# A streaming SiLU-gate kernel: first load cut in four, implied waits dropped, another closing wait

## The chip, the cores and the metric

The kernel runs on one core of a Trainium2 chip. The metric is device time in microseconds. Three runs of the kernel before gave a median of 472.07 us (471.17 to 472.86). The profile is of one execution of 471.1 us, whose span (first to last instruction) is 469.2 us.

A core has compute engines with instruction queues of their own, of which this kernel uses ScalarE (ACT), VectorE (DVE) and, to issue transfers, SyncE (SP). Transfers between the main memory (HBM) and the on-chip memory (SBUF, 128 partitions) are carried by sixteen DMA engines. An instruction waits for others by semaphores; a transfer raises its semaphore when it has landed.

## The reference

The input x is 32 x 512 x 2048 in float32, 134.22 MB. Its last dimension is cut in halves; the first goes through SiLU and gates the second:

```
half_dim = x.shape[-1] // 2
x1, x2 = (x[..., :half_dim].copy(), x[..., half_dim:].copy())
silu_x1 = x1 * (1 / (1 + np.exp(-x1)))
return (silu_x1 * x2).astype(np.float32)
```

The output is 32 x 512 x 1024 in float32, 67.11 MB. Every element is read once and written once, with no reuse.

## The kernel before

The 16,384 rows are cut into 16 tiles of 128 x 8 rows: partition p of a tile holds eight consecutive rows, 64 KB of input and 32 KB of output, each contiguous in HBM. Two input tiles (xt0, xt1) and two output tiles (ot0, ot1) alternate. SiLU is done in place in the first half of each row of the input tile (line 61, ACT); the product goes to the output tile (line 65, DVE).

The order of the work on each engine is the order of the program text (a manual schedule); the framework adds the semaphore waits that follow from which instruction touches which tile.

- SP issues the loads (line 57), one transfer of 8.39 MB for each tile. Load 0 and load 1 go out at once; load i+2 waits until the multiplication of tile i has freed its input tile, and for load i on the same tile.
- ACT does the SiLU and issues the stores, after the multiplication of the same tile, so a store stands between two activations in its queue.
- DVE does the multiplications. Before one it waits for the SiLU of its tile, for the load of that tile, for the store that last read the output tile, and for an earlier multiplication.

Tile 0 is treated apart: SiLU and product run in four pieces of two rows (FIRST, line 11), and five stores take strided sets of partitions (OPENING, line 16): every fourth partition, those halfway between, and all odd ones, with their rows split. Tiles 1 to 14 are done in one piece each (lines 81 to 86), and the last tile in two halves (LAST, line 13), each with a store of its own.

At the end an empty instruction on SP (line 96) waits for the last transfers but one store and for the last product, so that the framework's closing drain has few waits left to make.

The lines that the change and the steps of the prediction touch are the helpers load, silu, mul and store (lines 56 to 70), the first loads (72 and 73) and the closing (96 to 98).

Of the kernel before, what the change touches and what calls it, by code (L numbers as in the profile page):

```python
# [1 line left out]

# [4 lines left out]


K = 8

FIRST = [(0, 2), (2, 4), (4, 6), (6, 8)]

LAST = [(0, 4), (4, 8)]


OPENING = [
    (slice(0, None, 4), slice(0, 2)),
    (slice(2, None, 4), slice(0, 4)),
    (slice(2, None, 4), slice(4, None)),
    (slice(0, None, 4), slice(2, None)),  # L20
    (slice(1, None, 2), slice(None)),
]
SYNC = mybir.DependencyInfo(mybir.DependencyClass.Sync, mybir.DependencyReason.DATA)


@with_exitstack
def kernel(
    ctx: ExitStack,
    tc: tile.TileContext,
    x: bass.AP,  # L30
    out: bass.AP,
):
    nc = tc.nc
    P = nc.NUM_PARTITIONS

    x_flat = x.flatten_outer_dims()
    out_flat = out.flatten_outer_dims()
    num_rows, in_cols = x_flat.shape
    half = in_cols // 2
    dt = x_flat.dtype  # L40
    n_tiles = num_rows // (P * K)
    assert n_tiles * P * K == num_rows

    x_view = x_flat.rearrange("(n p k) d -> n p k d", p=P, k=K)
    out_view = out_flat.rearrange("(n p k) d -> n p k d", p=P, k=K)

    in_pool = ctx.enter_context(tc.tile_pool(name="in_pool", bufs=1))
    out_pool = ctx.enter_context(tc.tile_pool(name="out_pool", bufs=1))
    xts = [in_pool.tile([P, K, in_cols], dt, name=f"xt{j}") for j in range(2)]
    ots = [out_pool.tile([P, K, half], dt, name=f"ot{j}") for j in range(2)]  # L50

    ctx.enter_context(tc.manual_schedule())

    dmas = []

    def load(i):
        dmas.append(nc.sync.dma_start(out=xts[i % 2], in_=x_view[i]))  # L57

    def silu(i, a, b):
        x1 = xts[i % 2][:, a:b, :half]  # L60
        nc.scalar.activation(out=x1, in_=x1, func=mybir.ActivationFunctionType.Silu)  # L61

    def mul(i, a, b):
        xt = xts[i % 2]
        return nc.vector.tensor_mul(  # L65
            out=ots[i % 2][:, a:b], in0=xt[:, a:b, :half], in1=xt[:, a:b, half:]
        )

    def store(i, a, b):
        dmas.append(nc.scalar.dma_start(out=out_view[i][:, a:b], in_=ots[i % 2][:, a:b]))  # L70

    load(0)
    load(1)
    for a, b in FIRST:
        silu(0, a, b)
        mul(0, a, b)
    for ps, ks in OPENING:
        dmas.append(nc.scalar.dma_start(out=out_view[0][ps, ks], in_=ots[0][ps, ks]))
    load(2)

    for i in range(1, n_tiles - 1):
        silu(i, 0, K)
        mul(i, 0, K)
        store(i, 0, K)
        if i + 2 < n_tiles:
            load(i + 2)

    i = n_tiles - 1
    for a, b in LAST:
        silu(i, a, b)  # L90
        last_mul = mul(i, a, b)
    for a, b in LAST:
        store(i, a, b)


    seen = nc.sync.nop()
    for ins in [*dmas[-12:-1], last_mul]:
        tc.add_manual_dep(seen.ins, ins.ins.name, SYNC, reason="the closing waits")


# [1 line left out]
_INS = ['x']  # L102
_OUTS = [((32, 512, 1024), 'float32')]


# [23 lines left out]
```

## Time and profile before

| what | value |
|---|---|
| median of three runs | 472.07 us |
| profiled execution, its time and span | 471.1 us, 469.2 us |
| DVE busy | 139.4 us (30%), 20 instructions |
| ACT busy | 114.1 us (24%), 21 instructions |
| SiLU of a whole tile, mean | 7.03 us |
| product of a whole tile, mean | 8.69 us |
| load, issue to landing, least and median | 21.7 us, 41.9 us |
| store of a whole tile, issue to landing, median | 49.1 us |

The load's least, 21.7 us, is load 0's, which has the DMA engines to itself. The others share them with stores, and a transfer that is issued while others are queued waits behind them, so these times are mostly queueing. The page gives for each engine the time in which it executes, for the DMA the share of sixteen engines' time that their packets took. The name SPq, ACTq or DVEq in a row means the engine's instruction queue: it waits, or issues a transfer, and the engine itself stays idle.

### The profile page before, as it was taken

Reading aid. Unit: us, or ns where it says so; the run is one execution under the profiler, and the core shown is the slowest. Engines: PE = TensorE matmul, PEld = TensorE weight load, DVE = VectorE, ACT = ScalarE, POOL = GpSimd, SP = SyncE. Lnnn points to the kernel's source line nnn. Section 1 sums busy time; section 2 is a strip of 40 time slices with the busy share of each in tenths; the row PEclk is TensorE's granted clock in tenths of the full one; section 3 lists DMA queues with packets and bytes.
Section 4 is the critical chain, followed back from the end, with each engine's and each line's share of the span. In section 5 each row is a group of like instructions: output and inputs, shape, how many; then the busy total and the mean of one; then the engine's idle time right before and its main releaser. Section 6 shows DMA issues by size and latency. Waiting matters only on the chain.

```text
span 469.2 us, 199 instructions
## 1 busy us (share of the span) xinstructions
DVE 139.4 (30%) x20; ACT 114.1 (24%) x21; POOL 0.2 (0%) x4
## 2 busy tenths in 40 slices
DVE  0070604207052060510606115060250702407061
ACT  1052305050140501405023050230503205032060
POOL 0000000000000000000000000000000000000000
DMA  8999999999999999999999999999999899999998
GB/s 358 447 469 425 397 453 399 405 492 402 447 402 492 402 402 447 486 408 402 447 425 469 402 444 405 447 447 413 436 492 436 369 447 486 408 448 399 422 430 358
DMA packets 4881, 201.34 MB, mean 429 GB/s; under 512 B 592, under 2 KB 592, under 8 KB 592
## 3 DMA queue, kind: packets, MB, share of 16 engines
q1 hardware_dynamic: 2304, 134.22, 66.3%
q10 hardware_dynamic: 2576, 67.11, 33.2%
q14 instruction: 1, 0.01, 0.0%
HBM read 134.22 MB, written 67.11 MB: 429 GB/s over the span
## 4 chain that ended last, share of the span: by engine, by line
DMA 80%; DVE 14%; ACT 2%; DVEq 1%; issue 0%; SPq 0%; ACTq 0%
DMA out_dram<-ot 62%; DMA xt<-in_x_dram 18%; DVE ot L65 14%; ACT xt L61 2%; DVEq L124 1%; DVEq L65 0%; SPq L57 0%; ACTq L61 0%
## 5 line engine op out<-in xcount | busy, mean ns | idle before, releaser
L65 DVE TENSOR_TENSOR ot<-xt 128x8192 f32<-128x8192 f32 (+2 forms) x20 | 139.4, 6984 | 319.8 <-DMA out_dram<-ot 200.2
L61 ACT ACTIVATE xt<-xt 128x8192 f32<-128x8192 f32 (+2 forms) x20 | 112.9, 5662 | 338.9 <-DMA xt<-in_x_dram 338.9
L61 ACT ACT_TABLE_LOAD x1 | 1.3, 1283 | 0.7 <-PEq L113 0.7
L113 POOL MEMSET const-bfloat16-1.0<- 128x1 bf16 x1 | 0.1, 102 | 0.0
L113 POOL MEMSET const-uint8-127<- 128x1 uint8 x1 | 0.1, 102 | 0.0
L113 POOL MEMSET const-float32-0.0<- 128x1 f32 x1 | 0.1, 99 | 0.2 <-issue 0.2
L113 POOL MEMSET const-float32-1.0<- 128x1 f32 x1 | 0.1, 99 | 0.0
## 6 DMA issues: line engine op xcount, KB each, us to landing
out_dram<-ot ACTq DMA_DIRECT2D x14, 4096.0 KB, 49.1
out_dram<-ot ACTq DMA_DIRECT2D x3, 2048.0 KB, 9.2
out_dram<-ot ACTq DMA_DIRECT2D x2, 512.0 KB, 17.1
out_dram<-ot ACTq DMA_DIRECT2D x1, 768.0 KB, 27.9
xt<-in_x_dram SPq DMA_DIRECT2D x16, 41.9
out_dram<-ot ACTq DMA_DIRECT2D x1, 256.0 KB, 10.8
```

What stands on the lines that cost most here:

```text
L61: nc.scalar.activation(out=x1, in_=x1, func=mybir.ActivationFunctionType.Silu)
L65: return nc.vector.tensor_mul(out=ots[i % 2][:, a:b], in0=xt[:, a:b, :half], in1=xt[:, a:b, half:])
L113: nc = _bacc.Bacc("TRN2", target_bir_lowering=False, num_devices=1)
L124: with _tile.TileContext(nc) as tc:
```

## The change

- Load 0 becomes four transfers (ARRIVING): every eighth partition from 0, every eighth from 4, every fourth from 2, and all odd ones, that is 16, 16, 32 and 64 partitions. Each has a semaphore of its own, and the first SiLU waits for all four. Load 1 is issued behind them on SP.
- Waits that another wait implies are declared unnecessary: a multiplication no longer waits for its load (its SiLU did), nor for older work on the same tiles; likewise loads and activations. Some waits on older transfers appear elsewhere, where the framework still asks for them.
- An activation on a tile of one column (warm) stands ahead of everything on ACT. That tile takes 4 bytes in each partition ahead of the output tiles, which come to lie 32 bytes further on.
- The closing has two empty instructions on SP instead of one: the first waits for the last SiLU, the second for what the old one waited for. The closing drain then has the last store itself to wait for.

```
+ARRIVING = [slice(0, None, 8), slice(4, None, 8), slice(2, None, 4), slice(1, None, 2)]
...
+    def implied(ins, others):
+        for other in others:
+            tc.declare_no_dep(ins.ins, other.ins, reason="another wait implies it")
     def load(i):
-        dmas.append(nc.sync.dma_start(out=xts[i % 2], in_=x_view[i]))
+        for ps in ARRIVING if i == 0 else [slice(None)]:
+            ins = nc.sync.dma_start(out=xts[i % 2][ps], in_=x_view[i][ps])
+            dmas.append(ins)
+            loads.setdefault(i, []).append(ins)
+            if i >= 2:
+                implied(ins, [*loads[i - 2], *silus[i - 2]])
     def silu(i, a, b):
...
+        if i >= 2:
+            implied(ins, [*silus[i - 2], *muls[i - 2]])
     def mul(i, a, b):
...
+        implied(ins, loads[i])
+        if i >= 2:
+            implied(ins, [*loads[i - 2], *silus[i - 2], *muls[i - 2]])
...
+    warm = in_pool.tile([P, 1], dt, name="warm")
+    nc.scalar.activation(
+        out=warm,
+        in_=nc.const_aps.tensor(0.0, (P, 1), dt),
+        func=mybir.ActivationFunctionType.Silu,
+    )
     load(0)
     load(1)
...
-    seen = nc.sync.nop()
-    for ins in [*dmas[-12:-1], last_mul]:
-        tc.add_manual_dep(seen.ins, ins.ins.name, SYNC, reason="the closing waits")
+    for group in ([last_silu], [*dmas[-12:-1], last_mul]):
+        seen = nc.sync.nop()
+        for ins in group:
+            tc.add_manual_dep(seen.ins, ins.ins.name, SYNC, reason="the closing waits")
```

More of the change, by code (lines that the diff above doesn't have):

```diff
@@ L54 @@
     dmas = []
+    loads, silus, muls = {}, {}, {}
+    def implied(ins, others):
+        for other in others:
+            tc.declare_no_dep(ins.ins, other.ins, reason="another wait implies it")
     def load(i):
-        dmas.append(nc.sync.dma_start(out=xts[i % 2], in_=x_view[i]))
+        for ps in ARRIVING if i == 0 else [slice(None)]:
[4 more added lines that the diff above has]
+                implied(ins, [*loads[i - 2], *silus[i - 2]])
     def silu(i, a, b):
         x1 = xts[i % 2][:, a:b, :half]
-        nc.scalar.activation(out=x1, in_=x1, func=mybir.ActivationFunctionType.Silu)
+        ins = nc.scalar.activation(out=x1, in_=x1, func=mybir.ActivationFunctionType.Silu)
+        silus.setdefault(i, []).append(ins)
+        if i >= 2:
+            implied(ins, [*silus[i - 2], *muls[i - 2]])
+        return ins
     def mul(i, a, b):
         xt = xts[i % 2]
-        return nc.vector.tensor_mul(
+        ins = nc.vector.tensor_mul(
             out=ots[i % 2][:, a:b], in0=xt[:, a:b, :half], in1=xt[:, a:b, half:]
         )
+        muls.setdefault(i, []).append(ins)
+        implied(ins, loads[i])
+        if i >= 2:
+            implied(ins, [*loads[i - 2], *silus[i - 2], *muls[i - 2]])
+        return ins
     def store(i, a, b):
         dmas.append(nc.scalar.dma_start(out=out_view[i][:, a:b], in_=ots[i % 2][:, a:b]))
+    warm = in_pool.tile([P, 1], dt, name="warm")
[4 more added lines that the diff above has]
+    )
     load(0)
@@ L89 @@
     for a, b in LAST:
-        silu(i, a, b)
+        last_silu = silu(i, a, b)
         last_mul = mul(i, a, b)
```

## The prediction

> **What bounds the kernel now.** I read the page's DMA rows first, because both compute engines are idle most of the time (DVE 30%, ACT 24% busy). The page, its slices and its DMA rows:
>
> ```profile
> DMA  8999999999999999999999999999999899999998
> ...
> q1 hardware_dynamic: 2304, 134.22, 66.3%
> q10 hardware_dynamic: 2576, 67.11, 33.2%
> ...
> HBM read 134.22 MB, written 67.11 MB: 429 GB/s over the span
> ```
>
> Loads (q1) take 66.3% and stores (q10) 33.2% of sixteen engines' time over the span: together 99.5%. Nothing in the middle can be won by compute; only the two ends of the span and the pace of the packets are left. So I read the pace by stretches next (the columns are length, busy time of DVE, ACT and POOL, clock, DMA share, GB/s):
>
> ```profile
> 1.15:22.50 21.35, 0.00 (x0) 0.87 (x2) 0.00 (x0) 1.00 1.05 442
> 22.50:76.60 54.10, 17.59 (x5) 21.37 (x6) 0.00 (x0) 1.00 1.00 426
> 76.60:192.60 116.00, 34.77 (x4) 28.12 (x4) 0.00 (x0) 1.00 1.00 434
> ...
> 424.90:469.20 44.30, 17.45 (x3) 7.12 (x2) 0.00 (x0) 1.00 0.93 402
> ```
>
> The steady pace is 434 GB/s. A transfer's bytes count where its packets start, so the first row reads high and the last low. The second row holds the five strided stores of tile 0, and at 426 GB/s it lost 54.10 x (1 - 426/434) = 1.0 us. Then the same view, cut finely at the start:
>
> ```profile
> 1.70:1.80 0.10, 0.00 (x0) 0.10 (x1) 0.00 (x0) 1.00 9.66 3277
> 1.80:1.95 0.15, 0.00 (x0) 0.15 (x1) 0.00 (x0) 1.00 8.03 2621
> 1.95:2.20 0.25, 0.00 (x0) 0.06 (x1) 0.00 (x0) 1.00 0.72 262
> 2.20:2.50 0.30, 0.00 (x0) 0.00 (x0) 0.00 (x0) 1.00 1.12 437
> 2.50:2.80 0.30, 0.00 (x0) 0.00 (x0) 0.00 (x0) 1.00 1.05 437
> ...
> 4.60:5.00 0.40, 0.00 (x0) 0.00 (x0) 0.00 (x0) 1.00 2.27 983
> 5.00:5.20 0.20, 0.00 (x0) 0.00 (x0) 0.00 (x0) 1.00 7.56 3277
> ```
>
> A load's packet is one partition's 65,536 bytes, so GB/s times length counts packets: 5, 6, 1, 2 and 2 start in the first five rows (sixteen engines, one each, spread over 1.1 us), and 6 and 10 second packets start at 4.60 to 5.20. At 434/16 = 27.1 GB/s an engine needs 2.42 us for a packet. Second packets start at about 5.05 in the mean, so the streams ran as if begun at 5.05 - 2.42 = 2.63, though the first packet started near 1.75: some 0.9 us of lag. Last, the chain of waits (start, us, what) and the timeline, for one round of the loop:
>
> ```profile
> 105.53 0.03 issue
> 105.56 0.02 DVEq L65
> ...
> 105.72 8.70 DVE ot L65
> 114.43 0.02 issue
> 114.45 49.09 DMA out_dram<-ot
> ```
>
> ```profile
> 114.44 0.33 SPq L57 DMA_DIRECT2D xt<-in_x_dram  x1
> 114.45 0.36 ACTq L70 DMA_DIRECT2D out_dram<-ot  x1
> 127.44 7.03 ACT L61 ACTIVATE xt<-xt 128x8192 f32<-128x8192 f32 x1 [22.01 <-DMA xt<-in_x_dram]
> ```
>
> The chain names the multiplication, but it is not the limit: when it ends and SP issues the next load at 114.44, the load before it has 13 us of packets left (its silu starts at 127.44). The queue never runs dry.
>
> **The change part by part.** The sum is against the profiled execution: span 469.2, time 471.1, that is 0.97 below the median of 472.07 and at the low end of its runs (471.17 to 472.86).
>
> *First load in four.* Transfers of 16, 16, 32 and 64 partitions replace one of 128; bytes and packets stay. The first carries one packet for each of sixteen engines instead of eight, so I expect the late starters (five after 1.95) to start with the early ones. The earliest second packets start between 4.60 and 5.00, say 4.7, and the mean was 5.05: if all engines follow the earliest, the streams gain 0.35 us. Ends: 0 (the spread is not due to the transfer's size) and 0.9 (the whole lag goes). I take 0.35, since it supposes only what the quickest engines already show. This gain would last: the engines have no idle time behind it to absorb it.
>
> The price of the strided pattern on a load is in no row, since every load now spans 128 partitions. The nearest row is the stretch of strided stores (every fourth partition, every second): 1.0 us for five of them, 0.2 each. Ends: 0, and by bytes 8.39/4.19 x 1.0 = 2.0 us. I take 0.2, one such loss: the first transfer begins inside the start-up lag, and the stores lost it between alternating reads and writes, which the first load is not.
>
> Three more SP issues at 0.33 to 0.42 us move load 1's issue from 1.15 to about 2.4. Its packets are needed when engines leave load 0's, near 21.6, so 19 us cover it; without cover it would be 1.2 us. The next SP wait, for load 2, ends on the fourth multiplication at 33.4 as now. The first silu waits for four semaphores instead of one, some 0.05 us for each wait by the DVEq gaps above; the 21 us of load 1 hide 0.15 us.
>
> *Waits dropped.* From the landed store at 105.53 to the multiplication at 105.72 are 0.19 us of semaphore waits; one of two waits goes, some 0.1 us a round, 14 rounds. Load packets cover it (13 us a round), so I count nothing; were the cover gone it would be 1.4 us. Who is late next is again the DMA engines.
>
> *Warm activation.* The table load stays at 0.73 to 2.01. By 7.03 us for 8192 elements and 1.90 for 2048, an activation has about 0.2 us of fixed cost; ACT is idle until 22.49. Nothing. The small tile shifts the output tiles by 32 bytes in each partition. No row has that shift; stores hold 33.2% of the engines' time, 156 us, so one part in a thousand of their pace would be 0.16 us either way. I take 0.
>
> *Closing.* The last store is issued at 459.13 and lands 9.2 us later, at 468.4; the tail after it is 0.8 us. One semaphore wait of 17 ns with its gap leaves that tail: 0.05 us (ends 0 and 0.1). The last silu's wait moves ahead, to an instruction that it reaches with the activations done since 453.8; it delays nothing.
>
> Sum: -0.35 + 0.2 - 0.05 = -0.2 us on 471.1, that is 470.9; on the median 471.9.
>
> **The rivals.** Within 0.3%, 1.4 us, a measurement of this kernel can hardly tell a change from none.
>
> *Engines meet in SBUF (slower).* Sixteen engines write sixteen partitions that lie eight apart. If two must share one way in, each packet takes twice 2.42 us, and in lockstep every engine meets the same in the second transfer. Price: two packets an engine, 4.84 us, so 476.7. If the third and fourth transfers meet too, eight packets: 19.3 us, 491.2. It decides once the sixteen-partition packets take a third longer (1.6 us over both, to outweigh the 0.2 gained). Against it: strided stores at half speed would have cost 4.19 MB / 217 GB/s - 4.19 / 434 = 9.7 us, and that stretch lost 1.0. For it: those stores are reads of SBUF, every fourth partition and not every eighth. I give 0.19 to two slow transfers, 0.08 to four.
>
> [...]
>
> *The strided price goes by bytes.* 2.0 us instead of 0.2: 473.7, just slower. For it: the stretch at 426. Against: its cost need not repeat when only loads run. 0.09.
>
> *The whole lag and the strided stores' loss go.* Starts at once (0.9), arrival in another order also frees the stretch of its 1.0, and the tail gives 0.1: 470.1, faster by 0.4%. For it: both losses are in the rows. Against: five stores are unchanged. Or the dropped waits count after all, 1.4 us: about 470.5. Together 0.21.
>
> **How the numbers follow.** My forecast of 471.9 has 0.43, its own range 471.0 to 473.0. Slower is 0.19 + 0.08 + 0.09 = 0.36, faster 0.21, within 0.3% 0.43. The range runs from 469.9 (the faster rival and a little) to 477.2 (two slow transfers with half the strided price); it leaves out the four slow transfers and the low tail, some 0.15.
>
> **What would show it.** Second packets starting together at 4.6 to 4.8 prove the gain at the start; a first silu near 22.2 proves that nothing was lost in load 0. A first silu near 27 shows two slow transfers, near 41 four, with 217 GB/s from 2 to 12 us. The loop's pace must stay at 434 and the wait before a multiplication shrink by 0.1 us with no change in the spacing of stores. I am wrong if load 0 lands late, or if the output tiles' shift changes the pace of the steady stretches.

## The result, and the profile after

The changed kernel takes 475.36 us in the median of six runs (475.25 to 475.51). The kernel before, in more runs than the prediction had, takes 471.12. The runs of the kernel before lie in two groups, most near 471.0 and the rest 0.6 to 2.1 us above, so its median moves by some tenths of a microsecond with the share of each. The ratio is 1.0085, with a 95% interval of 1.0075 to 1.0095: slower by 0.85%, about 4.2 us. The profiled execution took 475.34 us with a span of 473.6.

The slices of the page, first the rates of the kernel before, then the changed kernel's busy shares and rates. The DMA engines are as full as before and the bytes are the same, but the first slice moves 194 GB/s instead of 358. A share counts the time that packets take, so slow packets don't show in it.

```profile
GB/s 358 447 469 425 397 453 399 405 492 402 447 402 492 402 402 447 486 408 402 447 425 469 402 444 405 447 447 413 436 492 436 369 447 486 408 448 399 422 430 358
```

```profile
DMA  8999999999999999999998999999999999998998
GB/s 194 426 443 400 432 453 421 437 426 443 443 443 443 443 399 443 443 407 435 487 443 376 437 471 399 443 443 443 399 443 440 446 404 437 487 437 379 426 440 354
```

The start of the changed kernel, cut finely (length, busy DVE, ACT, POOL, clock, DMA share, GB/s counted where a packet starts; the rows left out between 3.30 and 14.60 are zero):

```profile
1.70:1.95 0.25, 0.00 (x0) 0.25 (x1) 0.00 (x0) 1.00 0.00 0
1.95:3.30 1.35, 0.00 (x0) 0.26 (x2) 0.00 (x0) 1.00 3.56 777
...
6.30:7.80 1.50, 0.00 (x0) 0.00 (x0) 0.00 (x0) 1.00 3.30 699
7.80:11.20 3.40, 0.00 (x0) 0.00 (x0) 0.00 (x0) 1.00 0.00 0
11.20:12.80 1.60, 0.00 (x0) 0.00 (x0) 0.00 (x0) 1.00 1.85 655
...
14.60:15.40 0.80, 0.00 (x0) 0.00 (x0) 0.00 (x0) 1.00 3.03 1311
```

GB/s times length, divided by 65,536 bytes, is 16 in each row that is not zero: the engines go in step. Their second packets start at 6.3 to 7.8 (before: 4.6 to 5.2), the third at 11.2 to 12.8, the fourth at 14.6 to 15.4. From the middle of one row to the middle of the next are 4.95 us for the second packet, which is the one of the second transfer, where 2.42 is the steady time (65,536 bytes at 434/16 GB/s); the third takes 3.0 and later ones 2.4. Sixteen packets of 65,536 bytes in 4.95 us are 212 GB/s, half of 434. The first transfer fares the same, from about 2.4 to 7.05 with the start-up lag in it. The other two run at full pace but for the mixed third packet.

Nothing starts before 1.95; before the change, eleven engines had started by then. The chain (start, us, what) shows a part of the reason: the first issue, of a strided transfer, takes 0.58 us, where the old one took 0.37. The first row is the kernel before; the others are the changed kernel, the last two from a round of the loop, where the store has landed at 110.09 and the multiplication starts at 110.18.

```profile
0.73 0.37 SPq L57
```

```profile
0.73 0.58 SPq L69
...
1.37 0.57 SPq L69
...
110.09 0.03 issue
...
110.18 8.70 DVE ot L85
```

The timeline then gives the bill. The first SiLU starts at 28.00, where it started at 22.49; the SiLU of the third whole tile starts at 102.97, where it started at 98.41. First the kernel before, then the changed kernel:

```profile
22.49 5.51 ACT L61 ACTIVATE xt<-xt 128x2048 f32<-128x2048 f32 x3 [20.48 <-DMA xt<-in_x_dram]
...
98.41 7.03 ACT L61 ACTIVATE xt<-xt 128x8192 f32<-128x8192 f32 x1 [21.93 <-DMA xt<-in_x_dram]
```

```profile
28.00 5.51 ACT L77 ACTIVATE xt<-xt 128x2048 f32<-128x2048 f32 x3 [25.77 <-DMA xt<-in_x_dram]
...
102.97 7.03 ACT L77 ACTIVATE xt<-xt 128x8192 f32<-128x8192 f32 x1 [21.93 <-DMA xt<-in_x_dram]
```

So load 0 costs 5.51 us, the stretch with the strided stores gives 0.95 back (74.97 from SiLU to SiLU instead of 75.92), the rest of the span some 0.16, and what lies outside the span some 0.16: together 4.24, the difference of the two profiled executions.

The steady loop is unchanged, at the 434 GB/s of before:

```profile
81.20:197.20 116.00, 34.81 (x5) 28.12 (x4) 0.00 (x0) 1.00 1.00 434
```

### The profile page after: what moved, and what is told of

Same layout as the page of the kernel before. It is cut to its first block, busy times and chain, and to the rows that moved or that the text cites. A ratio compares the mean times of both kernels' runs of the same rounds, so it can differ in the third digit from the quotient of the medians.

```text
span 473.6 us, 177 instructions
## 1 busy us (share of the span) xinstructions
DVE 139.3 (29%) x20; ACT 114.3 (24%) x22; POOL 0.2 (0%) x4
## 4 chain that ended last, share of the span: by engine, by line
DMA 80%; DVE 14%; ACT 2%; DVEq 1%; SPq 0%; issue 0%
DMA out_dram<-ot 61%; DMA xt<-in_x_dram 19%; DVE ot L85 14%; ACT xt L77 2%; DVEq L157 1%; SPq L69 0%; DVEq L85 0%
```

## Which part costs: the parts alone

Three theories stood. "Engines meet", a supposition of the author's: two engines share one way into SBUF when sixteen partitions lie eight apart. "A cold start in small pieces is slow". "The other parts cost". Four kernels tell them apart.

**Load 0 whole, the rest of the change kept.**

```
-ARRIVING = [slice(0, None, 8), slice(4, None, 8), slice(2, None, 4), slice(1, None, 2)]
+ARRIVING = [slice(None)]
```

> The changed kernel with load 0 in one transfer again; the dropped waits, the warm activation, the shifted output tiles and the new closing stay. Theory 'engines meet' (two engines share one way into SBUF when sixteen partitions lie eight apart): the whole loss was in load 0, so this is at or below the kernel before, first silu near 22.4, and 470.0 to 471.1. It also says where the 0.9 us went that the strided stores no longer lose in the changed kernel: if that gain comes from these other parts, 470.1 and the stretch after load 0 at 430 GB/s or more; if it came from the engines' other order of arrival, 471.0 and 426 GB/s. Rival 'the other parts cost' (dropped waits or shifted tiles slow the loop): over 472.

Measured: 470.71 us against 471.24 for the kernel before, ratio 0.9983 (0.9973 to 0.9994), first SiLU at 22.60. The other parts cost nothing, and this version is the fastest of the study, though ahead of the kernel before by a sixth of a per cent only (the lowest runs of each are 470.54 and 470.91). From the first SiLU to that of the third whole tile it takes 75.78 us, nearly the 75.92 of before: the 0.95 us do not come from the other parts.

**The four transfers alone, on the kernel before.**

```
-        dmas.append(nc.sync.dma_start(out=xts[i % 2], in_=x_view[i]))
+        for ps in ARRIVING if i == 0 else [slice(None)]:
+            dmas.append(nc.sync.dma_start(out=xts[i % 2][ps], in_=x_view[i][ps]))
```

> The kernel before with only the four transfers for load 0. Engines meet: first silu near 27.9, 16 second packets start only 4.8 us after the first, 475.4 if the gain at the strided stores belongs to the split, 476.3 if it belongs to the other parts. The other parts cost: below 472.

Measured: 475.64 us, ratio 1.0084 (1.007 to 1.0098). The split is the whole loss, and it also brings the gain that follows. One thing more shows in its timeline, in which the first SiLU has several semaphores to wait for and nothing stands ahead of it:

```profile
27.82 1.28 ACT L63 ACT_TABLE_LOAD   x1 [27.82 <-DMA xt<-in_x_dram]
29.11 5.51 ACT L63 ACTIVATE xt<-xt 128x2048 f32<-128x2048 f32 x3
```

The table load now stands behind the waits, and the SiLU starts 1.28 us later. The warm activation prevents that (with it the table load stays at 0.73). With 475.64 against 475.36 us, measured on different chips, it makes no difference here that could be told from noise; the likely reason is that load 1 keeps the DMA engines busy meanwhile.

**Every fourth, those halfway, the odd ones.**

```
+ARRIVING = [slice(0, None, 4), slice(2, None, 4), slice(1, None, 2)]
```

> The changed kernel with load 0 in three transfers: every fourth partition, those halfway, the odd ones (32, 32, 64). Engines meet: every fourth partition spreads evenly, no packet over 3.4 us, first silu 22.4 to 23.0 (the first issue takes 0.58 us instead of 0.37), time within 0.6 us of the kernel with load 0 whole. Rival 'a cold start in small pieces is slow' (the loss comes from the first transfers being small and strided, whichever partitions they take): a first silu of 25 or later and 473 or more.

Measured: 470.89 us, ratio 0.9987 (0.9976 to 0.9997), first SiLU at 23.08. Strided transfers as such are not slow, nor is a cold start in pieces; what is left is a later start, 23.08 against 22.60, just above the expected 23.0.

**The four transfers in the opposite order.**

```
+ARRIVING = [slice(1, None, 2), slice(2, None, 4), slice(4, None, 8), slice(0, None, 8)]
```

> The changed kernel with the four transfers in the opposite order: odd partitions, every fourth, then the two of sixteen partitions last. Engines meet: the two slow packets an engine come at 17 to 27 us instead of 2 to 12, first silu again near 27.5, time 475.0 to 475.5. A cold start in small pieces is slow: the sixteen-partition transfers run warm and cost nothing, first silu near 22.8, time 470.5 to 471.5.

Measured: 475.75 us, ratio 1.009 (1.0075 to 1.0104), first SiLU at 28.54, both somewhat above the expectation of "engines meet" and far from the other. The windows of this kernel show the slow packets, now at the end of load 0; in the long rows hardly one starts (197 KB are three packets, 65 KB one):

```profile
16.30:17.60 1.30, 0.00 (x0) 0.00 (x0) 0.00 (x0) 1.00 2.89 655
17.60:20.50 2.90, 0.00 (x0) 0.00 (x0) 0.00 (x0) 1.00 0.32 68
20.50:22.60 2.10, 0.00 (x0) 0.00 (x0) 0.00 (x0) 1.00 2.18 468
22.60:25.20 2.60, 0.00 (x0) 0.00 (x0) 0.00 (x0) 1.00 0.12 25
25.20:27.60 2.40, 0.00 (x0) 0.00 (x0) 0.00 (x0) 1.00 1.16 410
```

The same two transfers are as slow when the engines have been running for 17 us: from the middle of one full row to that of the next are 4.6 and 4.85 us. "A cold start" falls.

## Which partitions: the disputed cost by itself

Every eighth partition could still be slow because a transfer has sixteen partitions, one packet for each engine. Two kernels hold the number, the size and the place, and differ in the partitions alone. Both have load 0 whole and one extra transfer ahead of it, whose bytes are loaded again with load 1:

```
+LEAD = slice(0, None, 8)      # the other kernel: slice(32, 96, 4)
...
+    nc.sync.dma_start(out=xts[1][LEAD], in_=x_view[1][LEAD])
     load(0)
```

> The changed kernel with load 0 whole, and ahead of it one extra transfer of sixteen partitions, every eighth from 0, into the other input tile (these bytes are loaded again with load 1; nothing is left out). It costs 2.42 us an engine at full pace. Engines meet, two to a way into SBUF: its sixteen packets take 4.8 us, so 470.7 + 4.8 = 475.5, or 474.7 if the strided stores then lose nothing, as in the runs with slow packets. Rival 'transfers of sixteen separate partitions are slow, whichever they are': the same 475.5 here.

> The same with the extra transfer's sixteen partitions taken four apart, 32 to 92: the same number, size and place, other partitions. [...] Engines meet: the packets take 2.42 us beside the start-up lag, 470.7 + 2.4 = 473.1. Sixteen separate partitions are slow whichever they are: 475.5, as with every eighth.

Measured: 475.07 us for every eighth, ratio 1.0089 (1.0075 to 1.0103); 473.57 for every fourth from 32, ratio 1.006 (1.0047 to 1.0072). First every eighth, then every fourth: where the first and the second packets start.

```profile
1.70:3.30 1.60, 0.00 (x0) 0.51 (x2) 0.00 (x0) 1.00 3.04 655
...
6.50:7.80 1.30, 0.00 (x0) 0.00 (x0) 0.00 (x0) 1.00 2.22 807
```

```profile
1.70:3.30 1.60, 0.00 (x0) 0.51 (x2) 0.00 (x0) 1.00 1.91 655
...
5.10:5.50 0.40, 0.00 (x0) 0.00 (x0) 0.00 (x0) 1.00 6.09 2622
```

Sixteen packets start in each of these rows, and none in between. With every fourth all second packets start by 5.5, with every eighth none before 6.5. The first SiLU starts at 25.14 and at 27.74: 2.6 us for the choice of the partitions. The whole differs by 1.5 us only, mostly since the stretch behind load 0 gives 0.94 back after the slow packets (next section). So 475.07 lies between the two values offered for it, and 473.57 is 0.5 above the expectation. It is which partitions, not how many.

That the sixteen from 32 on would run at full pace was the author's supposition before the run.

**Neighbouring partitions.** The last one asks whether sixteen partitions side by side lose more than sixteen that lie eight apart. The expectation's 19.4 us for the first two packets and 29.0 us for the six behind them are four times and twice the steady 2.42; both factors were the author's supposition, which no run before this one showed for such sets.

```
+ARRIVING = [slice(0, 16), slice(16, 32), slice(32, 64), slice(64, None)]
```

> The changed kernel with the same four sizes as blocks of neighbouring partitions: 0 to 15, 16 to 31, 32 to 63, 64 to 127. [...] Load 0 lasts 19.4 + 29.0 = 48.4 us instead of 19.3, first silu near 51, time near 499. If what counts is only that a transfer has sixteen partitions, the first two alone are slow: 475.4.

Measured: 499.55 us, ratio 1.0606 (1.0587 to 1.0625), first SiLU at 52.31. The windows, again with sixteen packets in each row and none in between:

```profile
1.70:3.30 1.60, 0.00 (x0) 0.51 (x2) 0.00 (x0) 1.00 5.26 655
...
8.90:11.30 2.40, 0.00 (x0) 0.00 (x0) 0.00 (x0) 1.00 3.91 437
...
18.30:20.60 2.30, 0.00 (x0) 0.00 (x0) 0.00 (x0) 1.00 2.47 456
```

From 10.1 to 19.45, the middles of two rows, are 9.35 us for the second packet: nearly four times 2.42. The block of 64 neighbours is slow too, at 206 GB/s from 30 to 50 us, so it isn't the small number of partitions.

The loss goes by the set of partitions. The sixteen from 32 to 92 show none: they put the first SiLU 2.54 us behind that of load 0 whole, where a packet at the steady pace takes 2.42. Nor do the three transfers of the kernel with every fourth (470.89 us, against 470.71 with load 0 whole). Every eighth takes twice 2.42 for a packet (4.95), sixteen neighbours nearly four times (9.35).

In all these kernels a partition and its 64 KB in HBM go together, so the runs by themselves show that the choice of rows decides, and not on which side, HBM or SBUF, the time is lost. A wide stride in HBM is not what costs: the rows of every eighth partition lie 512 KB apart there and those of every fourth 256 KB, but the slowest, the neighbours, lie back to back. That engines share a way into SBUF stays the author's supposition: the runs show how long a packet takes, not what it waits for.

## Where 0.95 us came back

In the changed kernel the stretch of the strided stores is 0.95 us shorter, about the 1.0 us that the prediction read as lost there. Time from the first SiLU to that of the third whole tile, from the timelines (one profile each) of the kernels whose stores follow the first SiLU alike, with the number of slow packets that each engine had in load 0 or ahead of it:

| kernel | slow packets | us |
|---|---|---|
| before | none | 75.92 |
| load 0 whole | none | 75.78 |
| every fourth, halfway, odd | none | 75.61 |
| extra transfer, every fourth from 32 | none | 75.98 |
| changed kernel | two | 74.97 |
| opposite order | two | 74.77 |
| extra transfer, every eighth | one | 75.04 |
| neighbouring blocks | all | 74.81 |

Those with slow packets are shorter by 0.6 to 1.2 us. Four more runs asked why. "Clash" stands here for a transfer over a set of partitions that showed slow packets above.

A short clash (two rows of every eighth partition, 16 KB) and the same without a clash (two rows of every fourth from 32):

```
-    nc.sync.dma_start(out=xts[1][LEAD], in_=x_view[1][LEAD])
+    nc.sync.dma_start(out=xts[1][LEAD, 0:2], in_=x_view[1][LEAD, 0:2])
```

> Load 0 whole, and ahead of it a short extra transfer: two rows (16 KB) of every eighth partition, loaded again later. Where does the strided stores' loss of about 0.9 us go in the runs with slow packets? Theory 'phase': a clash at the start leaves the sixteen engines in another order, and the stores then do not get in each other's way. Then the short clash does it too: 0.6 us for the bytes, 0.6 for the clash, 0.9 back, 471.0, the stretch of the strided stores at full pace. Rival 'only the delay of load 0 by five microseconds does it': the loss stays, 471.9.

> [...] Both theories: no clash, 0.6 us for the bytes, the strided stores lose as before, 471.3.

Measured: 471.60 us (ratio 1.0006, 0.9998 to 1.0015) and 471.67 (1.0018, 1.0008 to 1.0028); 75.96 and 75.91 us from SiLU to SiLU. The short clash does not do it. It hardly was one: the extra transfer lands half a microsecond later with it (load 1, which waits for that, is issued at 4.26 instead of 3.75), but the first SiLU starts at 23.56 and 23.51. So this pair leaves the theory of phases open.

The delay without a clash, by two extra transfers of every fourth from 32 and from 33:

```
-LEAD = slice(32, 96, 4)
+LEAD = [slice(32, 96, 4), slice(33, 96, 4)]
```

> Load 0 whole, and ahead of it two extra transfers of sixteen partitions four apart (from 32 and from 33), loaded again later: load 0 is delayed by 4.8 us as in the runs with slow packets, but without a clash. Theory 'a long clash reorders the engines' (the strided stores lose nothing only after it): the loss after load 0 stays at 0.6 to 0.9 us, 470.7 + 4.8 = 475.5 to 476.0. Rival 'the delay alone does it': no packet after load 0 over 2.43 us, 474.7 to 475.1.

Measured: 475.77 us, ratio 1.0105 (1.0089 to 1.0122), first SiLU at 27.69, 75.73 us from SiLU to SiLU. As late as the changed kernel, and the loss stays. The delay alone is ruled out; a long clash goes with the gain in four kernels of four, and no kernel without one has it. By what means it comes stays open.

The strided stores replaced by three over all partitions:

```
 OPENING = [
-    (slice(0, None, 4), slice(0, 2)),
...
+    (slice(None), slice(0, 2)),
+    (slice(None), slice(2, 4)),
+    (slice(None), slice(4, None)),
 ]
```

> Load 0 whole and the rest of the change kept, and the five strided stores of tile 0 replaced by three over all 128 partitions (rows 0 and 1, 2 and 3, 4 to 7). If the loss after load 0 belongs to the strided pattern, the stretch runs at 434 GB/s and the time is 469.8 to 470.0; if it belongs to stores that begin there, whatever their pattern, 470.7.

Measured: 473.39 us, ratio 1.0055 (1.0039 to 1.0072), worse than either expectation. The timeline of this kernel:

```profile
91.00 8.69 DVE L83 TENSOR_TENSOR ot<-xt 128x8192 f32<-128x8192 f32 x1 [31.37 <-DMA out_dram<-ot]
99.72 0.33 SPq L67 DMA_DIRECT2D xt<-in_x_dram  x1
```

Loads ran ahead of stores: from 27 to 66 us loads and stores had 256 and 240 packets and moved 14.68 and 1.84 MB, where with the strided stores (load 0 whole) 225 and 208 packets moved 13.70 and 2.62 MB. In both kernels the two had nearly equal numbers of packets, and here the store packets are smaller (1.84 MB in 240 packets, against 2.62 in 208). The multiplication of tile 2 waited for a store until 91.00 (76.62 in the kernel before), and the next load was issued only at 99.72. From 88 to 100 us no load moved a byte, and at 100 to 104 us the DMA moved 262 GB/s:

```profile
100.00:104.00 4.00, 0.00 (x0) 3.87 (x1) 0.00 (x0) 1.00 0.92 262
```

The run doesn't tell what causes the loss at the strided stores. It shows what they are worth: the queue of loads, which the prediction called never dry, did run dry here.

## Why the prediction was wrong

The forecast was 471.9, within 0.3% of before, with 0.43; slower had 0.36. Measured is 475.36, slower by 4.2 us. It lies inside the range (469.9 to 477.2) only because the range was drawn up to a rival; the forecast itself had load 0 a little quicker, and it came 5.5 us later. Point by point:

- **The bound** was right. The DMA engines are the limit, and what load 0 loses is paid in full: extra bytes alone (+2.42 us, every fourth from 32) cost 473.57 - 470.71 = 2.86 us, twice of them 475.77 - 470.71 = 5.06 (good to about 0.3 us, since these kernels ran on different chips and the kernel before, run beside each, had medians from 470.96 to 471.24).
- **"The price of the strided pattern on a load", taken as 0.2 us, is the step that failed.** Two transfers of sixteen partitions cost some 5 us, mostly as two packets an engine at half pace (4.95 us where 2.42 is the steady time). The row used, the strided stores, covers every fourth and every second partition, and the kernel with every fourth shows that such sets run at full pace as loads too. It said nothing of every eighth. The rival "engines meet in SBUF" had the time, 4.84 us for two transfers, from a supposition that no run shows directly. It was given 0.19, with the strided stores held against it, although the prediction adds there that they take every fourth partition and not every eighth.
- **The gain at the start, 0.35 us, failed in sign.** The late starters do not come from the size of the transfer: a transfer of sixteen partitions starts its engines over 1.95 to 3.30, as spread out as one of 128. And with a strided transfer first everything starts later, by some 0.35 us: 0.48 at the first SiLU of the kernel with every fourth. The longer issue is 0.2 of that; the rest stays open. It goes with the stride and not with the size: in the kernel with neighbouring blocks, whose first transfer has sixteen partitions too and is issued in 0.38 us, nine packets start before 1.95. (By the middles of the rows shown, the second packets' mean is 4.99 and not 5.05, so the term was 0.3 on its own reading.)
- **The dropped waits** were right: from 0.19 to 0.09 us in each round (110.09 for the landed store, 110.18 for the multiplication), and worth nothing that the runs can tell, since loads cover it.
- **Warm, the shift by 32 bytes, the SP issues**: nothing that costs, as said; with load 0 whole the warm activation, the shift, the dropped waits and the new closing together measure 0.9983. Where that sixth of a per cent comes from was not tried part by part. The issues took longer than assumed, so load 1 was issued at 3.25 and not at 2.4, which its cover of 19 us hides.
- **The closing**: 0.05 us was forecast and can't be seen. The last store is issued at 463.28 and lands 9.3 us later at 472.6, and the span ends at 473.6: the tail is 1.0 us, where it was 0.8.
- **The rival's 476.7** was 1.3 too high: 0.95 us came back behind load 0, which no case had together with it, and the median of before that it was set on, 472.07, came down to 471.12 with more runs. Against that, load 0 came 5.51 us later, where 4.84 was counted. So the rival had the doubled time of a packet, and its number is close in part by errors that cancel.

## What to carry to other kernels

When a load is cut by partitions, look at which partitions each piece has, not at how many: here every fourth partition ran at full pace, every eighth at half (4.95 us for a packet, where 2.42 is the steady time), and a block of sixteen neighbours at about a quarter (9.35). A row that looks like the new operation bounds it only if it shares the property that decides; the strided stores had no set of every eighth partition, so their rows were no evidence against the rival. In this kernel, which is bound by transfers, a first load in one piece of all partitions was as good as any cut that was tried.

## What was not expected of the hardware

- With a transfer over strided partitions first, as in the changed kernel, SP takes 0.58 us to issue it and the first packet starts after 1.95 us; with one over all partitions first, as in the kernel before, 0.37 and near 1.75. The pattern alone does not decide: load 1 of the changed kernel, over all partitions and right behind a strided transfer, took 0.59 too.
- In the one kernel whose first activation had several semaphores to wait for and no warm activation ahead of it, the table load came behind the waits (27.82 instead of 0.73).
- One or more slow packets of 4.6 to 9.35 us on each engine, in load 0 or ahead of it, go with 0.6 to 1.2 us less in the stretch of the strided stores behind them. Cause open.
